# VectorE computes every low part of the weight chunks of a two-layer mixer kernel; GpSimd computes none

## The chip, the cores and the metric

The kernel runs on one core of a Trainium2 chip. Its time is the device time of one launch in microseconds (us), median of several runs. The engines of the core work side by side: TensorE (PE, matrix products into PSUM), VectorE (DVE), ScalarE (ACT), GpSimd (POOL), and SyncE (SP), which here only issues DMAs. A trace lists TensorE's loading of weights apart, as PEld.

## The reference, cut to what matters

Two streams of 256 tokens by 2048 features, `x` and `ctx`, go through two layers; all data is float32. Each layer projects the normalised tokens by wide weight matrices, mixes, and projects back.

```python
def _even_mixer(h_x, h_c, w_in, ..., w_out):            # layer 0
    # projections h @ w_in, then a short convolution and silu of q, k, v
    for d in range(2):                                   # forwards and backwards
        oc_d, s_ctx = _gdn_chunk_scan(q_c, k_c, v_c, ...)     # context first
        ox_d, _ = _gdn_chunk_scan(q_x, k_x, v_x, ..., s_ctx)  # then x, from the context's state
    ...
def _gdn_chunk_scan(q, k, v, g, beta, s0):
    m = strict_lower(kb @ k.T * decay)
    t_inv = inverse(eye + m)                             # per head and chunk: a triangular solve
    ...                                                  # then, chunk by chunk:
    v_new = u_i - w_i @ S;  o = qg_i @ S + a_i @ v_new;  S = S * gl + kg_i.T @ v_new
def _odd_stream(...):                                    # layer 1: gelu, token mixing, pooling
    return concatenate([y_c, y_d]) @ w_out
```

## The kernel before, in words

**High and low parts.** TensorE is fed numbers in a rounded format (fp32r in the trace). To keep float32's precision each operand is split in two: a high part H, the rounded copy, and a low part L, the rest (operand minus H). A projection is then three products: H by H, H by L, and L by H. The activations are split once; the weights arrive from memory in chunks of 128 x 1024 numbers (512 KB; 128 x 768 in the first stage), and each chunk is split when it arrives, by the helper `wchunk`:

```python
raw = (rp or wrawp).tile([P, sz], F32, name="raw", tag="raw")
dma(raw, src)
H = ...tile([P, sz], F32R, name="H", tag="H")
S.copy(H, raw)                                  # L202, ScalarE
L = ...tile([P, sz], F32R, name="L", tag="L")
tick[3] += LP[tick[2]]
if tick[3] >= 1.0:
    tick[3] -= 1.0
    G.tensor_tensor(L, raw, H, ALU.subtract)    # L207, GpSimd
else:
    V.tensor_tensor(L, raw, H, ALU.subtract)    # L209, VectorE
```

`raw`, `H` and `L` have four buffers each. `LP` is a table of shares, one for each stage (`tick[2]` is the stage's number): with 0.5 every second chunk's L goes to GpSimd, with 0.2 every fifth. `RATE` beside it sets how many steps of the layers' modulation vectors (`ada_step`, VectorE's multiply-add L277 with a 256 KB load) come with each chunk.

**The stages.** (0) Normalisation and the first projections (matmuls L450), then keys and values (`wkv`): the matmuls L230, a convolution on VectorE (L351 to L363) whose result TensorE transposes (L599). (1) Four groups of four heads, in one loop. Each group projects q and z, builds per head the matrices U from products E (L747, L749) with VectorE's L757 and L759, then **solves**: 30 steps of elimination on VectorE, each a product (L779, into `ltmp`) and a sum (L781, into `LB`), with transposes around them (L773, L774, L786 to L789) and copies L798 into `UT`. Then the **chain**: TensorE's PT (L807), XT and X (L815, L819, L835, L845) finish the inverse with copies on ScalarE and VectorE between them, and the scan goes through eight steps: z (L883), zk on ScalarE (L887), Sp (L894), the state St on VectorE (L899), kS and QS (L863, L871), r on VectorE (L866), and again z, up to the transposes oT (L922). Beside it, the group's share of sixteen blocks `wbb` is projected (matmuls L230) and convolved. After the fourth group the first part of the output projection starts (L239, L240, L241: H by H, L by H and H by L, 512 columns). (2) The rest of the output projection of layer 0 and the norm. (3) Layer 1.

**What sets the order.** The code is written stage by stage, but a scheduler in the tile framework puts the instructions of each engine in an order of its own before the program is built (`schedule_with_timeline_sim=True`), by its own costs and by what each operation depends on; the solve and the scan have priority (`tc.high_priority()`). On the chip each engine then runs its list strictly in order: an instruction that waits holds up all behind it on the same engine. So the projections' matmuls that stand on TensorE's list between E and PT are what TensorE has to do while VectorE solves.

Of the kernel before, what the change touches and what calls it, by code (L numbers as in the profile page):

```python
# [30 lines left out]
LA = 4  # L31
FINK = 2
RATE = (2.5, 0.6, 1.2, 0.4)
LP = (0.5, 0.5, 0.4, 0.2)
CHUNKS = (1, 2, 4, 4, 5)
RADII = (1, 2, 4, 8)

# [85 lines left out]
def body(ctx: ExitStack, tc: tile.TileContext, T, dbg=None):  # L123
# [71 lines left out]
    def wchunk(src, nk, rp=None, hp=None, lp=None, sz=1024, HL=None):  # L195
# [7 lines left out]
        L = HL[1] if HL else (lp or wlp).tile([P, sz], F32R, name="L", tag="L")  # L203
        tick[3] += LP[tick[2]]
        if tick[3] >= 1.0:
# [989 lines left out]
```

## Time and profile before

| What | Value |
|---|---|
| Median of 3 runs (lowest, highest) | 2234.3 us (2229.0, 2234.8) |
| The profiled execution: time, span of its trace | 2233.2 us, 2231.4 us |
| TensorE busy, share of the span | 2091.3 us, 94% |
| VectorE | 1521.7 us, 68% |
| ScalarE | 995.0 us, 45% |
| GpSimd | 548.3 us, 25% |
| Granted TensorE clock, mean | 0.972 of full speed |
| L on GpSimd (L207) | 205 of 128 x 1024 or less, 508.8 us |
| L on VectorE (L209) | 349, 446.5 us |

Busy time counts the time in which an instruction of the engine was under way, also when that instruction was held up after its start. A share of the whole span is a mean over stages with different limits, so tables over stretches of time are more use than this one. The granted clock tells how much of full speed TensorE had in a stretch.

### The profile page before, as it was taken

To read this page: it belongs to the slowest core of one execution; us is meant where nothing else is said; L and a number is where in the kernel's file an instruction comes from. 1 tells how busy PE (TensorE), PEld (TensorE's weight loads), DVE (VectorE), ACT (ScalarE), POOL (GpSimd) and SP (SyncE) were. 2 spreads that over 40 slices of the span, in tenths; PEclk is the share of its full clock that TensorE was granted. 3 is DMA by queue.
4 is the path that set the end of the run, shared out by engine and by line. 5 is a ranking of instruction groups with operands and counts; after the bars stand their busy time and mean duration, and the time that the engine had idled before them with its cause. 6 is when DMAs were issued, how large, how long until landed. Compare 5 with 4: busy or idle time off the path is not lost. (4 is left out here: it accounts for less than half of the span.)

```text
span 2231.4 us, 42172 instructions
## 1 busy us (share of the span) xinstructions
PE 2091.3 (94%) x17034; PEld 1946.6 (87%) x17034; DVE 1521.7 (68%) x2500; ACT 995.0 (45%) x1726; POOL 548.3 (25%) x258
## 2 busy tenths in 40 slices
PE   6999899999989988998999887999999999999998
PEld 4789899898989988998898876787799999999886
DVE  4337986778965996599569953886767675545445
ACT  5233264225554544563555363445454444444343
POOL 1112111123322332233233321342122112221221
PEclk9999999999999998999899999999999999999999
DMA  9777455767445753564457553896866666666664
GB/s 342 259 264 231 153 166 171 231 210 244 141 133 170 238 187 125 174 210 144 121 187 235 180 166 117 296 317 217 290 202 206 179 184 199 183 191 223 193 194 133
DMA packets 151267, 446.41 MB, mean 200 GB/s; under 512 B 16512, under 2 KB 23456, under 8 KB 150048
## 3 DMA queue, kind: packets, MB, share of 16 engines
q1 hardware_dynamic: 145936, 425.37, 59.4%
q0 software_dynamic: 5136, 18.35, 2.6%
q8 instruction: 133, 2.18, 0.4%
q14 instruction: 62, 0.51, 0.1%
HBM read 423.19 MB, written 20.46 MB: 199 GB/s over the span
## 5 line engine op out<-in xcount | busy, mean ns | idle before, releaser
L202 ACT CAST H<-raw 128x1024 fp32r<-128x1024 f32 (+1 forms) x554 | 573.1, 1042 | 690.1 <-PE pj L230 326.2
L207 POOL TENSOR_TENSOR L<-raw,H 128x1024 fp32r<-128x1024 f32 (+1 forms) x205 | 508.8, 2483 | 1511.1 <-ACT H L202 1426.1
L209 DVE TENSOR_TENSOR L<-raw,H 128x1024 fp32r<-128x1024 f32 (+1 forms) x349 | 446.5, 1281 | 351.3 <-ACT H L202 348.8
L230 PE MATMUL pj<-hxH,L 128*128 128x256 f32 x1856 | 538.1, 290 | 32.5 <-DVE L L209 32.4
L230 PE MATMUL pj<-hxH,H 128*128 128x256 f32 x1856 | 537.0, 289 | 0.1
L230 PE MATMUL pj<-hxL,H 128*128 128x256 f32 x1856 | 536.0, 289 | 0.0
L230 PEld LDWEIGHTS pj<-hxH,L 128*128 128x128 f32 x1856 | 361.7, 195 | 38.7 <-DVE L L209 35.8
L230 PEld LDWEIGHTS pj<-hxL,H 128*128 128x128 f32 x1856 | 361.4, 195 | 2.4 <-issue 1.2
L230 PEld LDWEIGHTS pj<-hxH,H 128*128 128x128 f32 x1856 | 361.3, 195 | 1.8 <-issue 0.9
L230 PE MATMUL pj<-h1H,H 128*128 128x256 f32 x1024 | 291.2, 284 | 0.2 <-DVE yo L1055 0.2
L230 PE MATMUL pj<-h1L,H 128*128 128x256 f32 x1024 | 290.5, 284 | 0.0
L230 PE MATMUL pj<-h1H,L 128*128 128x256 f32 x1024 | 290.3, 284 | 0.0
L277 DVE SCALAR_TENSOR_TENSOR acc<-araw,cs,acc 128x512 f32<-128x512 f32 x240 | 242.8, 1012 | 42.1 <-DMA araw<-in_ada 24.2
L230 PEld LDWEIGHTS pj<-h1H,H 128*128 128x128 f32 x1024 | 197.2, 193 | 0.5 <-PE adc L287 0.3
L230 PEld LDWEIGHTS pj<-h1L,H 128*128 128x128 f32 x1024 | 197.2, 193 | 0.1
L230 PEld LDWEIGHTS pj<-h1H,L 128*128 128x128 f32 x1024 | 197.2, 193 | 0.0
L230 PE MATMUL pj<-hcL,H 128*128 128x256 f32 x320 | 90.9, 284 | 0.0
L230 PE MATMUL pj<-hcH,L 128*128 128x256 f32 x320 | 90.8, 284 | 0.0
L230 PE MATMUL pj<-hcH,H 128*128 128x256 f32 x320 | 90.8, 284 | 0.0
L239 PE MATMUL pj<-H,y1H 128*128 128x512 f32 x192 | 76.0, 396 | 0.0
L241 PE MATMUL pj<-H,y1L 128*128 128x512 f32 x192 | 75.9, 396 | 0.0
L240 PE MATMUL pj<-L,y1H 128*128 128x512 f32 x192 | 75.9, 395 | 0.0
(433 smaller groups left out, 3843.0 us busy)
## 6 DMA issues: line engine op xcount, KB each, us to landing
raw<-in_wbb SPq DMA_DIRECT2D x128, 512.0 KB, 3.9
raw<-in_wout SPq DMA_DIRECT2D x128, 512.0 KB, 4.5
araw<-in_ada SPq DMA_DIRECT2D x192, 256.0 KB, 4.6
raw<-in_ada SPq DMA_DIRECT2D x64, 512.0 KB, 6.3
raw<-in_wpz SPq DMA_DIRECT2D x64, 512.0 KB, 4.1
raw<-in_wuz SPq DMA_DIRECT2D x64, 512.0 KB, 4.1
raw<-in_wkv SPq DMA_DIRECT2D x40, 512.0 KB, 4.4
araw<-in_ada0g SPq DMA_DIRECT2D x64, 256.0 KB, 4.1
```

What stands on the lines that cost most here:

```text
L202: S.copy(H, raw)
L207: G.tensor_tensor(L, raw, H, ALU.subtract)
L209: V.tensor_tensor(L, raw, H, ALU.subtract)
L230: PE.matmul(o[:, e * 256:(e + 1) * 256] if m > 1 else o, w, a[t][:, k, :], start=st and i == 0 and e == 0, stop=sp and i == 2, skip_group_ ...
L239: PE.matmul(o, xH[:, t], H[:, kk, :], start=st, stop=False, skip_group_check=True)
L240: PE.matmul(o, xH[:, t], L[:, kk, :], start=False, stop=False, skip_group_check=True)
L241: PE.matmul(o, xL[:, t], H[:, kk, :], start=False, stop=sp, skip_group_check=True)
L277: V.scalar_tensor_tensor(aacc[u // KT], raw, cs[:, k, 0:1], aacc[u // KT], ALU.mult, ALU.add)
```

## The change

One line: the shares of the table go to zero in all four stages, so `wchunk` takes its second branch for every chunk.

```diff
-LP = (0.5, 0.5, 0.4, 0.2)
+LP = (0.0, 0.0, 0.0, 0.0)
```

All 207 subtractions of GpSimd's list (205 into `L`, two into `h1L`) become subtractions of VectorE's; GpSimd keeps its DMAs (L688, L666, L1108 to L1123, L1147) and six products at the end (L1153). The same numbers are computed. But the scheduler orders all engines anew, since its costs for VectorE's list change.

VectorE, in the solve of the first group: L779 and L781 are the elimination's product and sum (their sizes grow and shrink with the step), L209 the chunks' low parts, L934 and L351 and L352 belong to the convolution of a `wbb` block. Before:

```order
L779 TENSOR_TENSOR ltmp<-LB 128x184
L209 TENSOR_TENSOR L<-raw,H 128x1024
L781 TENSOR_TENSOR LB<-LB,ltmp 128x23x8
L779 TENSOR_TENSOR ltmp<-LB 128x198
L781 TENSOR_TENSOR LB<-LB,ltmp 128x22x9
L779 TENSOR_TENSOR ltmp<-LB 128x210
L934 TENSOR_TENSOR cg<-cg,pj 128x256
L781 TENSOR_TENSOR LB<-LB,ltmp 128x21x10
L779 TENSOR_TENSOR ltmp<-LB 128x220
L351 SCALAR_TENSOR_TENSOR cbt<-cg,cols,cbt 128x4x63
```

VectorE, the same place, now:

```order
L209 TENSOR_TENSOR L<-raw,H 128x1024
L781 TENSOR_TENSOR LB<-LB,ltmp 128x24x7
L779 TENSOR_TENSOR ltmp<-LB 128x184
L781 TENSOR_TENSOR LB<-LB,ltmp 128x23x8
L779 TENSOR_TENSOR ltmp<-LB 128x198
L209 TENSOR_TENSOR L<-raw,H 128x1024
L781 TENSOR_TENSOR LB<-LB,ltmp 128x22x9
L779 TENSOR_TENSOR ltmp<-LB 128x210
L781 TENSOR_TENSOR LB<-LB,ltmp 128x21x10
L209 TENSOR_TENSOR L<-raw,H 128x1024
L779 TENSOR_TENSOR ltmp<-LB 128x220
```

Three or four steps of the elimination stand between two low parts instead of seven to ten. Between the last U (L757) and the first UT (L798) of a group VectorE's list has 8, 10, 9 and 10 low parts in the four groups before, and 21, 29, 23 and 22 now.

TensorE, in the scan of the fourth group (ybH and ybL are activations, H and L the weight chunks of the output projection). Before, the triples L239, L240, L241 stand between the scan's matmuls, up to the last third of the scan:

```order
L241 MATMUL pj<-H,ybL 128x512
L883 MATMUL z<-r,U 128x128 x4
L239 MATMUL pj<-H,ybH 128x512
L240 MATMUL pj<-L,ybH 128x512
L241 MATMUL pj<-H,ybL 128x512
```

TensorE, the same scan, now:

```order
L883 MATMUL z<-Vn,U 128x128 x4
L894 MATMUL Sp<-zk,Kt 128x128
L883 MATMUL z<-Vn,U 128x128 x4
L894 MATMUL Sp<-zk,Kt 128x128 x7
L863 MATMUL kS<-St,KTt 128x128 x4
L883 MATMUL z<-r,U 128x128 x4
L894 MATMUL Sp<-zk,Kt 128x128
L863 MATMUL kS<-St,KTt 128x128 x4
```

From the first PT to oT of the fourth group TensorE's list had 34 matmuls L230 and 192 of L239 to L241 between those of the chain; now it has none. They stand earlier: on TensorE's list between the last E and the first PT of a group there were 455, 536, 454 and 538 matmuls L230, and now there are 584, 753, 609, and in the fourth group 190 of L230 and the 192 of L239 to L241.

## The prediction

> **What bounds the kernel now.** I read the page first, then who TensorE waits for, then stretches of time, then VectorE's list around one wait.
>
> ```profile
> PE 2091.3 (94%) x17034; PEld 1946.6 (87%) x17034; DVE 1521.7 (68%) x2500; ACT 995.0 (45%) x1726; POOL 548.3 (25%) x258
> ```
>
> TensorE carries the span, so a change that touches VectorE and GpSimd alone can only act on what TensorE loses: waits, and stretches at a lower clock. First the waits of TensorE in the four groups but for the last chain (540 to 1290 us), then in all that follows:
>
> ```profile
> PE pj L230 <- DVE L L209: 32.4, 15, 5.1
> PE PT L807 <- DVE UT L798: 15.5, 4, 5.3
> ...
> PE pj L239 <- ACT h1H L345: 2.5, 1, 2.5
> PE pj L240 <- DVE L L209: 2.4, 1, 2.4
> ```
>
> TensorE waits for low parts, but for VectorE's, never for GpSimd's; and after the groups there is next to nothing to gain or to lose, because the waits listed there (1398 to 2232 us) come to 7 us. Now the stretches. Columns: us, then busy us and number of PE, PEld, DVE, ACT, POOL, then granted clock, DMA share and GB/s. In order: keys and values; the solves of the four groups (last E to first PT) with the chain and next projections between them; last the chain of the fourth group.
>
> ```profile
> 240.00:540.00 300.00, 279.05 (x2317) 274.61 (x2315) 236.52 (x433) 124.28 (x275) 64.37 (x28) 0.97 0.60 195
> 567.00:631.00 64.00, 56.40 (x456) 55.58 (x454) 61.40 (x104) 31.99 (x47) 21.86 (x9) 0.96 0.45 149
> 631.00:743.00 112.00, 108.67 (x1283) 106.16 (x1284) 64.15 (x118) 56.02 (x108) 33.23 (x16) 0.96 0.51 158
> 774.00:858.00 84.00, 70.40 (x545) 69.16 (x544) 82.20 (x123) 40.37 (x57) 29.70 (x11) 0.92 0.57 184
> 858.00:965.00 107.00, 104.49 (x1241) 102.32 (x1242) 61.27 (x122) 50.87 (x103) 28.57 (x14) 0.95 0.51 157
> 992.00:1062.00 70.00, 59.45 (x465) 58.10 (x464) 68.17 (x111) 34.50 (x49) 20.70 (x8) 0.93 0.47 151
> 1062.00:1177.00 115.00, 110.33 (x1296) 107.96 (x1297) 69.66 (x128) 55.80 (x110) 35.08 (x16) 0.95 0.53 164
> 1205.00:1289.00 84.00, 68.32 (x546) 67.01 (x544) 82.31 (x124) 37.22 (x55) 28.33 (x11) 0.95 0.57 187
> 1289.00:1398.00 109.00, 93.40 (x913) 80.94 (x916) 48.29 (x100) 49.74 (x94) 24.89 (x11) 0.91 0.44 140
> ```
>
> In the solves VectorE is busy 61.4 of 64, 82.2 of 84, 68.2 of 70 and 82.3 of 84 us: there it is the bound, and TensorE runs out of work. A matmul L230 follows the one before after 0.119 us at full clock, an L239 to L241 after 0.232:
>
> ```profile
> 600.08 0.28 PE L230 MATMUL pj<-hxH,H 128*128 128x256 f32 x1
> 600.20 0.28 PE L230 MATMUL pj<-hxL,H 128*128 128x256 f32 x1
> 600.32 0.28 PE L230 MATMUL pj<-hxH,L 128*128 128x256 f32 x1
> ...
> 1339.42 0.40 PE L239 MATMUL pj<-H,ybH 128*128 128x512 f32 x1
> 1339.66 0.39 PE L240 MATMUL pj<-L,ybH 128*128 128x512 f32 x1
> 1339.89 0.40 PE L241 MATMUL pj<-H,ybL 128*128 128x512 f32 x1
> ```
>
> So the solves hold 54, 65, 55 and 65 us of matmuls, and TensorE loses 10, 19, 15 and 19 us in them. What VectorE does there:
>
> ```profile
> 603.10 1.22 DVE L209 TENSOR_TENSOR L<-raw,H 128x1024 fp32r<-128x1024 f32 x1
> ...
> 606.44 0.41 DVE L781 TENSOR_TENSOR LB<-LB,ltmp 128x234 f32<-128x234 f32 x1
> 606.50 2.57 POOL L207 TENSOR_TENSOR L<-raw,H 128x1024 fp32r<-128x1024 f32 x1 [5.68 <-ACT H L202]
> 606.88 2.44 DVE L779 TENSOR_TENSOR ltmp<-LB 128x228 f32<-128x228 f32 x1
> 609.36 0.40 DVE L781 TENSOR_TENSOR LB<-LB,ltmp 128x228 f32<-128x228 f32 x1
> ```
>
> The product at 606.88 takes 2.44 us, the sum of the same size behind it 0.40: it ends when GpSimd's subtraction does. VectorE's operations with two inputs in SBUF stand still while GpSimd subtracts. What that costs in one solve (774 to 858 us, groups of rows with count, busy us and mean ns), with undisturbed rows behind:
>
> ```profile
> L781 DVE TENSOR_TENSOR LB<-LB,ltmp 128x30 f32<-128x30 f32 (+14 forms) x30 | 17.9, 598 | 0.6
> L779 DVE TENSOR_TENSOR ltmp<-LB 128x30 f32<-128x30 f32 (+14 forms) x30 | 13.9, 462 | 0.8
> L277 DVE SCALAR_TENSOR_TENSOR acc<-araw,cs,acc 128x512 f32<-128x512 f32 x12 | 13.1, 1093 | 0.0
> ...
> 797.50 0.20 DVE L779 TENSOR_TENSOR ltmp<-LB 128x30 f32<-128x30 f32 x1
> 797.95 0.75 DVE L277 SCALAR_TENSOR_TENSOR acc<-araw,cs,acc 128x512 f32<-128x512 f32 x1
> ```
>
> A step has 30 to 240 elements, 165 in the mean; between 0.20 and 0.41 us that is 0.33, so 60 of them take 20 us and took 31.8: 12 us lost; L277 loses 12 x 0.34 = 4 us. Operation by operation against the lower quartile of its own shape, this stretch loses 22 us (the rest lies in copies and convolution steps), the whole trace 228.
>
> **The change, part by part.**
>
> *GpSimd's 207 subtractions go.* None was ever waited for; the gain is what they did to VectorE, 228 us of its time. GpSimd's DMAs (L688, L666, L1121) lose what stood ahead of them on its list; nobody waits for them by the rows above, so 0.
>
> *VectorE gets 207 subtractions.* 1.22 us each, 252 us, less for the 16 small ones. Its sum rises from 1521.7 by some 20 us, and where it is the bound it falls: in the solve shown, eleven low parts moved cost 13.4 us and 22 us of standing still go.
>
> The Trainium skill (Perfetto Trace Analysis, Optimizing Scalar/DVE Operations) says that with VectorE saturated, offloading even to GpSimd may make sense, and adds that it might not help because the two share a read port. The 2.44 us row agrees with the addition; by the first half alone this change would load a saturated engine and end slower, which is the last rival below.
>
> *The first three solves.* VectorE's list between last U and first UT, at undisturbed durations: low parts 21, 29, 23 at 1.22, the elimination with its transposes and copies 32, L277 0, 13, 0 at 0.75, convolution 6, 12, 8: 63, 90 and 67 us. TensorE's matmuls there, 584, 753 and 609 at 0.119: 70, 90 and 72 us. So TensorE has enough to do, with no reserve in the second. It lost 44 us there; I leave 5 us each for low parts that come late, whose releaser would then be H. **-29**; ends -44 (no wait) and 0 (VectorE, whose low parts wait for H in order ahead of the elimination, keeps each wait).
>
> *After the solves.* The clock rows between the solves (0.96, 0.95, 0.95 of 112, 107, 115 us) show 15 us worth lost after the waits for low parts and PT. Half goes: **-8**; ends -15 and 0. But the second group's scan now ends, as the fourth's did, without matmuls between its steps; there the last wait for oT was 6.6 us, in the other groups together 4.1 us:
>
> ```profile
> PE oT L922 <- DVE on L919: 6.6, 1, 6.6
> ...
> PE oT L922 <- DVE on L919: 4.1, 3, 1.8
> ```
>
> **+6**; ends +2 and +8.
>
> *The fourth group.* Its solve: 22 low parts, 27 us, elimination 33, twelve L277 9, others 10, sum 78, and 3.5 of copies UT; the stretch was 84. TensorE has 190 x 0.119 + 192 x 0.232 = 67 us there, so VectorE still ends last: **-2**. The chain took 109 us with 34 x 0.119 + 192 x 0.232 = 49 us of other matmuls in it. Bare it is no shorter than 60, if all its waits were hidden already, and at most 75: the part that was bare took 34 us (first row below: covered, second: bare, with 13 us idle), the covered 75 us less 49 leave 26, and some 15 us of copies, zk, r and St come out from cover.
>
> ```profile
> 1289.00:1364.00 75.00, 72.66 (x771) 61.94 (x772) 32.43 (x51) 35.55 (x53) 20.18 (x9) 0.94 0.49 150
> 1364.00:1398.00 34.00, 20.74 (x144) 18.99 (x145) 15.86 (x49) 14.19 (x41) 4.72 (x2) 0.84 0.35 116
> ```
>
> I take 68, since both directions of the scan now alternate on TensorE's list and fill one another's waits: -41. The 45 us of matmuls that left this group (113 us before, 67 now, last E to oT) are run in the earlier groups and count there in full: **+45**. Ends of the chain with its clock: -8 and +18 around that.
>
> *Keys and values.* 25 low parts cost VectorE 31 us and give back about as much (L277 there has a mean of 1017 ns for 60, so 16 us, the rest elsewhere); VectorE is busy 236 of 300 us. **0**; ends -10 and +10, since TensorE's waits there are for the convolution. Output projection and layer 1: 0. Their cover is VectorE's spare time (rows below: busy 127 of 162 and 392 of 672 us); the 45 low parts moved after 1560 us add 55 us less what stood still, and without that spare time they would cost up to that. The first stage likewise: 0.
>
> ```profile
> L277 DVE SCALAR_TENSOR_TENSOR acc<-araw,cs,acc 128x512 f32<-128x512 f32 x60 | 61.0, 1017 | 17.4 <-DMA araw<-in_ada0g 9.0 <-DMA araw<-in_ada 7.5
> ...
> PE kvp L599 <- DVE kvT L363: 11.9, 6, 4.1
> ...
> 1398.00:1560.00 162.00, 159.17 (x745) 128.22 (x738) 127.31 (x161) 73.53 (x100) 58.58 (x26) 0.99 0.83 278
> 1560.00:2232.00 672.00, 656.39 (x4448) 606.76 (x4446) 392.09 (x520) 287.39 (x368) 133.05 (x73) 0.99 0.65 198
> ```
>
> Sum: -29 - 8 + 6 - 2 - 41 + 45 + 0 = -29, from the profiled execution's 2233.2 (1.8 us over its span, 1.1 under the median): **2204 us**. What is late next is UT, in the fourth group.
>
> **The rivals.**
>
> *No change.* The waits stay and only change their releaser: VectorE's list is in order, and a low part that waits for H holds the elimination behind it; before, half of those waits stood on GpSimd's list, where they hurt nobody. For it: in the second solve 90 us stand against 90. Against it: in the solve of 774 to 858 us VectorE waited for nothing (82.2 busy of 84). Without the 29 and the 8 it is 2233 + 6 - 2 - 41 + 45 = 2241; with a third of the gain, about 2230.
>
> *Slower, by the bare chain.* The chain's place is 1289 to 1398; if it takes 75 us and the clock of the bare stretch (0.84 and less) stretches its 40 us of matmuls by 10, the fourth group is +19 instead of +2, and if the 45 us moved ahead find waits in the earlier solves anyway (none of the 29), the time is 2233 + 19 + 6 = 2258. It decides once the earlier solves give back less than the chain loses, some 25 us. For it: nothing stands between the chain's matmuls. Against it: in the old order cover came in lumps of 21 matmuls that lengthened each step.
>
> *Much faster.* Keys and values also gain, as the scheduler's order meets an undisturbed VectorE: all lower ends together, 2233 - 44 - 15 + 2 - 6 - 10 = 2160. Against it: VectorE's sum there does not fall.
>
> *Slower, by load.* If rows like the 2.44 us one were rare, 39 moved low parts in the four solves would add 39 x 1.22 = 48 us where VectorE is the bound: 2281.
>
> **How the numbers follow.** A measurement of this kernel tells 0.3% from no change, about 7 us. Chances: my forecast (2185 to 2227) 0.47, much faster 0.13, no change 0.17, slower by the bare chain 0.18, by load 0.05. So faster 0.60, same 0.17, slower 0.23. The range leaves out a tenth at either side: 2160 to 2262; the forecast's own is 2185 to 2227.
>
> **What would show it.** Right: L277 falls from 1012 ns to 750 in the mean and VectorE's sum stays within 30 us of 1521.7; TensorE's wait for L209 in the groups falls from 32.4 to under 15 us; the fourth group's chain takes 60 to 75 us at a clock under 0.85, bare of L239. Wrong: waits for low parts whose H came late, an elimination that takes longer than 70 and 90 us, or a chain over 80 us.

## The result, and the profile after

The changed kernel takes **2155.8 us** (median of 4 runs, 2153.4 to 2160.6) where the kernel before, timed beside it, takes 2234.6 (2229.0 to 2237.1). The ratio is **0.965, 95% interval 0.963 to 0.968**: 79 us faster. The forecast was 2204 and the range 2160 to 2262; the direction is the one forecast, the time lies below the range. Two executions that were disturbed, one of the run with the first stage alone (4055 us) and the profiled one of the third lighter solve (5171 us), are left out of the figures below.

First the page's line of busy times of the changed kernel. Its profiled execution has a span of 2153.3 us, 78.1 less than before.

```profile
PE 2062.5 (96%) x17034; PEld 1922.4 (89%) x17034; DVE 1521.6 (71%) x2707; ACT 997.1 (46%) x1726; POOL 34.1 (2%) x51
```

VectorE runs 207 instructions more, and its busy time is the same to 0.1 us: what the low parts add is what the standing still beside GpSimd had cost. TensorE does the same 17034 matmuls in 28.8 us less, since a matmul is shorter at full clock, and it stands idle for 2153.3 - 2062.5 = 90.8 us where it was 140.1. These two, 29 and 49 us, are the whole gain. So the gain is TensorE's lost time, though the change touches neither its work nor its operands.

Whom TensorE waits for, over the whole trace after (total us, times, longest); the last two lines are all that is left of the waits for low parts and for the convolution of keys and values:

```profile
PE PT L807 <- DVE UT L798: 19.2, 6, 14.6
...
PE oT L922 <- DVE on L919: 13.1, 2, 6.6
PE pj L230 <- DVE zb L942: 3.8, 2, 3.0
...
PE pj L240 <- DVE L L209: 0.6, 1, 0.6
...
PE kvp L599 <- DVE kvT L363: 0.6, 1, 0.6
```

Before, the groups alone had 32.4 us for L209, and keys and values 11.9 us for L363. What is late now is UT, most of it in the fourth group (18.2 of the 19.2 us), as the forecast named it.

The stretches of time, with the columns as before (us; busy us and number of PE, PEld, DVE, ACT, POOL; granted clock; DMA share; GB/s). The first row begins where the row of keys and values before began, and ends, as that one did, at the first E. Then come solve and scan of the four groups in turn, and the beginning of layer 1, from TensorE's transposes of its normalised input (L1015) to VectorE's first silu (L1055):

```profile
240.00:516.50 276.50, 275.76 (x2357) 272.95 (x2355) 226.66 (x456) 124.89 (x275) 2.42 (x3) 1.00 0.66 217
545.00:614.00 69.00, 69.00 (x584) 68.83 (x582) 64.71 (x122) 40.19 (x54) 0.00 (x0) 1.00 0.57 171
614.00:722.00 108.00, 104.86 (x1271) 102.75 (x1270) 69.54 (x137) 53.25 (x107) 2.25 (x3) 0.98 0.54 169
750.00:842.00 92.00, 88.98 (x745) 88.65 (x744) 87.43 (x158) 50.93 (x66) 0.00 (x0) 0.98 0.70 219
842.00:938.00 96.00, 85.62 (x1093) 82.68 (x1092) 56.87 (x116) 43.10 (x90) 2.25 (x3) 0.96 0.48 151
966.00:1038.00 72.00, 72.00 (x608) 71.83 (x607) 67.82 (x125) 41.92 (x55) 0.00 (x0) 1.00 0.59 177
1038.00:1149.00 111.00, 106.53 (x1285) 104.28 (x1286) 69.24 (x135) 55.59 (x108) 2.24 (x3) 0.98 0.53 166
1180.00:1265.00 85.00, 67.73 (x366) 57.37 (x364) 75.66 (x132) 39.94 (x48) 0.75 (x1) 0.92 0.66 217
1265.00:1326.00 61.00, 43.11 (x684) 39.71 (x688) 29.22 (x81) 25.99 (x69) 0.00 (x0) 0.81 0.18 58
1464.00:1612.00 148.00, 145.92 (x883) 129.44 (x882) 113.61 (x181) 75.45 (x115) 8.80 (x16) 1.00 0.74 242
```

The last of these was, before:

```profile
1535.00:1690.00 155.00, 148.56 (x899) 130.75 (x897) 118.21 (x175) 77.39 (x120) 34.60 (x25) 1.00 0.72 231
```

Read the first row against its like: keys and values took 300 us with TensorE busy for 279 and now take 276.5 with TensorE busy for 275.8, at full clock. In the first three solves TensorE is busy for 230 of 233 us. By the starts of the same instructions in the two traces, the 78 us lie here:

| From | To | Before, us | After, us | Difference | Forecast |
|---|---|---|---|---|---|
| start | first matmul of keys and values into `kvp` (L599) | 251.0 | 250.7 | 0 | 0 |
| `kvp` | first E (L747) | 288.7 | 265.8 | **-23** | **0** |
| first E | first oT (L922) of the fourth group | 856.2 | 807.6 | **-49** | **-29** |
| oT | first L1015 | 139.4 | 139.9 | 0 | 0 |
| L1015 | first L1055 | 154.3 | 147.7 | **-7** | **0** |
| L1055 | end | 541.9 | 541.6 | 0 | 0 |

VectorE's groups after, then two of before (count, busy us, mean ns, idle before them). The elimination's product and sum fall from 528 and 518 ns to 328 and 329, and the multiply-add L277 from 1012 to 745:

```profile
L277 DVE SCALAR_TENSOR_TENSOR acc<-araw,cs,acc 128x512 f32<-128x512 f32 x240 | 178.8, 745 | 30.9 <-DMA araw<-in_ada 18.4 <-DMA araw<-in_ada0g 10.9
L781 DVE TENSOR_TENSOR LB<-LB,ltmp 128x30 f32<-128x30 f32 (+14 forms) x120 | 39.4, 329 | 2.1
L779 DVE TENSOR_TENSOR ltmp<-LB 128x30 f32<-128x30 f32 (+14 forms) x120 | 39.4, 328 | 2.1
```

```profile
L779 DVE TENSOR_TENSOR ltmp<-LB 128x30 f32<-128x30 f32 (+14 forms) x120 | 63.3, 528 | 3.2
L781 DVE TENSOR_TENSOR LB<-LB,ltmp 128x30 f32<-128x30 f32 (+14 forms) x120 | 62.2, 518 | 2.5
```

### The profile page after: what moved, and what is told of

It is laid out like the page before. It is cut to its first block, busy times and chain, and to the rows that moved or that the text cites. A ratio compares the mean times of both kernels' runs of the same rounds, so it can differ in the third digit from the quotient of the medians.

```text
span 2153.3 us, 42158 instructions
## 1 busy us (share of the span) xinstructions
PE 2062.5 (96%) x17034; PEld 1922.4 (89%) x17034; DVE 1521.6 (71%) x2707; ACT 997.1 (46%) x1726; POOL 34.1 (2%) x51
## 5 line engine op out<-in xcount | busy, mean ns | idle before, releaser
L209 DVE TENSOR_TENSOR L<-raw,H 128x1024 fp32r<-128x1024 f32 (+1 forms) x554 | 667.5, 1207 | 386.0 <-ACT H L202 370.1
L230 PE MATMUL pj<-hxH,H 128*128 128x256 f32 x1856 | 526.8, 284 | 3.8 <-DVE zb L942 3.8
L230 PE MATMUL pj<-hxH,L 128*128 128x256 f32 x1856 | 525.6, 283 | 0.0
L230 PE MATMUL pj<-hxL,H 128*128 128x256 f32 x1856 | 525.3, 283 | 0.0
L230 PEld LDWEIGHTS pj<-hxH,H 128*128 128x128 f32 x1856 | 350.7, 189 | 5.9 <-DVE zb L942 4.1
L230 PEld LDWEIGHTS pj<-hxH,L 128*128 128x128 f32 x1856 | 350.7, 189 | 2.3 <-issue 1.2
L230 PEld LDWEIGHTS pj<-hxL,H 128*128 128x128 f32 x1856 | 350.8, 189 | 0.9
L230 PE MATMUL pj<-h1H,H 128*128 128x256 f32 x1024 | 290.4, 284 | 0.0
L230 PE MATMUL pj<-h1L,H 128*128 128x256 f32 x1024 | 289.8, 283 | 0.0
L230 PE MATMUL pj<-h1H,L 128*128 128x256 f32 x1024 | 289.8, 283 | 0.0
L277 DVE SCALAR_TENSOR_TENSOR acc<-araw,cs,acc 128x512 f32<-128x512 f32 x240 | 178.8, 745 | 30.9 <-DMA araw<-in_ada 18.4
L230 PEld LDWEIGHTS pj<-h1H,H 128*128 128x128 f32 x1024 | 196.5, 192 | 0.2 <-ACT zg L1054 0.2
L230 PEld LDWEIGHTS pj<-h1L,H 128*128 128x128 f32 x1024 | 196.5, 192 | 0.1
L230 PEld LDWEIGHTS pj<-h1H,L 128*128 128x128 f32 x1024 | 196.5, 192 | 0.0
L230 PE MATMUL pj<-hcH,L 128*128 128x256 f32 x320 | 90.4, 283 | 0.0
L230 PE MATMUL pj<-hcH,H 128*128 128x256 f32 x320 | 90.4, 282 | 0.0
L230 PE MATMUL pj<-hcL,H 128*128 128x256 f32 x320 | 90.1, 281 | 0.0
L239 PE MATMUL pj<-H,y1H 128*128 128x512 f32 x192 | 76.0, 396 | 0.0
L241 PE MATMUL pj<-H,y1L 128*128 128x512 f32 x192 | 75.9, 396 | 0.0
L240 PE MATMUL pj<-L,y1H 128*128 128x512 f32 x192 | 75.9, 395 | 0.0
L230 PEld LDWEIGHTS pj<-hcH,L 128*128 128x128 f32 x320 | 60.1, 188 | 0.5 <-issue 0.4
```

Of the source, the lines that this page charges most:

```text
L230: PE.matmul(o[:, e * 256:(e + 1) * 256] if m > 1 else o, w, a[t][:, k, :], start=st and i == 0 and e == 0, stop=sp and i == 2, skip_group_ ...
L239: PE.matmul(o, xH[:, t], H[:, kk, :], start=st, stop=False, skip_group_check=True)
L240: PE.matmul(o, xH[:, t], L[:, kk, :], start=False, stop=False, skip_group_check=True)
L241: PE.matmul(o, xL[:, t], H[:, kk, :], start=False, stop=sp, skip_group_check=True)
L277: V.scalar_tensor_tensor(aacc[u // KT], raw, cs[:, k, 0:1], aacc[u // KT], ALU.mult, ALU.add)
```

## The experiments

"Standing still" below is the sum, over VectorE's operations beside an operation of GpSimd, of what each took beyond the median of its own shape when undisturbed: 228 us before, 4 after. All ratios are to the kernel before, with 95% intervals.

### GpSimd subtracts again, for nobody

This asks whether it is really GpSimd's work that costs, and not the order that the scheduler made of it. VectorE keeps all low parts; for each one that GpSimd used to have in the first stage and the first three groups it also subtracts into scratch (`jon[0]` is false from the fourth group on; the diff is cut).

```diff
+        n = tick[3] >= 1.0                 # tick[3] adds up the shares (0.5, 0.5, 0.4, 0.2)
+        tick[3] -= 1.0 * n
+        if n and jon[0]: G.tensor_tensor(<scratch, 128 x sz>, raw, H, ALU.subtract)
         V.tensor_tensor(L, raw, H, ALU.subtract)
```

> As e1, but GpSimd's useless subtraction is a whole one, as it was before the change (raw minus H, 128 x 1024 or 128 x 768, one instruction), written into a tile that is not in use until the fourth group; so it stands in the first stage and in the first three groups, for the chunks for which GpSimd computed the low part before. VectorE computes every low part. Theory A (standing still in proportion to the time that GpSimd reads): VectorE's multiply-add L277 in keys and values rises from 745 to about 1000 ns in the mean, waits of TensorE for kvT come back to 10 us or more there, the first E of the groups comes at 535 us or later instead of 516, and the time is 2225 to 2290 us, over e1 and, with 252 us more on VectorE, at or over the kernel before. Theory C (order): 2150 to 2190 us.

Measured: 2249.3 us, ratio 1.006 (1.004 to 1.009), so 94 us over the changed kernel in an order much nearer to the changed kernel's than to the one before (TensorE's list has 585, 841, 595 and 407 other matmuls between the last E and the first PT of a group, where the changed kernel has 584, 753, 609 and 382, and the kernel before 455, 536, 454 and 538). The page's line, TensorE's waits, and for 240 to 540 us the stretch and VectorE's multiply-adds:

```profile
PE 2094.2 (93%) x17034; PEld 1946.6 (87%) x17034; DVE 1677.1 (75%) x2707; ACT 993.1 (44%) x1726; POOL 328.7 (15%) x159
```

```profile
PE pj L230 <- DVE L L209: 40.4, 22, 4.8
...
PE kvp L599 <- DVE kvT L363: 15.2, 10, 6.0
```

```profile
240.00:540.00 300.00, 282.52 (x2353) 277.76 (x2352) 269.05 (x461) 123.81 (x274) 73.94 (x29) 0.98 0.60 198
```

```profile
L277 DVE SCALAR_TENSOR_TENSOR acc<-araw,cs,acc 128x512 f32<-128x512 f32 x65 | 67.0, 1031 | 13.1 <-DMA araw<-in_ada0g 7.5 <-DMA araw<-in_ada 5.0
```

294 us of GpSimd's subtractions, of which nobody reads a number, bring back 156 us of VectorE's busy time, the multiply-add at 1031 ns, the waits for low parts and the waits for `kvT`. The standing still is the cause, in keys and values too: the first E starts at 540.4 us (539.7 before, 516.5 in the changed kernel).

### Nobody does GpSimd's share

The other side: what do the 207 subtractions cost on VectorE? The kernel leaves these low parts out and gives TensorE the high part in their place; the diff is cut.

```diff
         if tick[3] >= 1.0:
             tick[3] -= 1.0
-            G.tensor_tensor(L, raw, H, ALU.subtract)
+            L = H
```

> The low parts that GpSimd computed before the change are computed by no engine: for these chunks TensorE is given the high part in place of the low part (the output is not the reference's). So GpSimd is idle as in the changed kernel and VectorE has 207 subtractions, 252 us, less. Theory A: what the change added to VectorE costs little, since VectorE has spare time outside the solves: 2110 to 2150 us, that is 5 to 45 us under the changed kernel, from the last solve and its wait for UT. If the load on VectorE were the price of the change, 2080 us or less. Theory B: about the changed kernel's time less the last wait, 2130 to 2156.

Measured: 2118.2 us, ratio 0.948 (0.946 to 0.951).

```profile
PE 2052.1 (97%) x17034; PEld 1916.1 (91%) x17034; DVE 1297.0 (61%) x2500; ACT 993.9 (47%) x1726; POOL 33.6 (2%) x51
```

VectorE's sum falls by 224.7 us against before, which is the standing still (228). Taking the work off GpSimd is worth 2232 - 2118 = 114 us; doing it on VectorE costs 2156 - 2118 = 38 us, though it is 225 us of work. One us of standing still cost 0.50 us of the time, one us of added subtraction 0.17. The order here is close to that of the kernel before, not to the changed one (460, 537, 448 and 542 matmuls L230 between the last E and the first PT of a group, where the kernel before has 455, 536, 454 and 538). So the 114 us are a gain almost without a new order, and the 38 us hold the new order as well as the subtractions. In keys and values the difference is the plainest: from the first `kvp` to the first E it takes 265.6 us with nobody, 265.8 with VectorE, 286.1 with the useless work on GpSimd and 288.7 before. There the added low parts cost nothing that can be seen.

### One stage at a time

```diff
-LP = (0.5, 0.5, 0.4, 0.2)
+LP = (0.0, 0.5, 0.4, 0.2)      # first stage alone
+LP = (0.5, 0.0, 0.4, 0.2)      # the four groups alone
+LP = (0.5, 0.5, 0.0, 0.0)      # the two last stages alone
```

> Shares 0.0, 0.5, 0.4, 0.2: only the first stage (first projections, keys and values) has its low parts all on VectorE. By the traces the first E of the groups comes 23 us earlier in the changed kernel. Theory A: that gain belongs to this stage alone, TensorE's waits for kvT are gone there: 2200 to 2212 us. If the gain of the stage came from the order of the whole program, it need not appear: 2225 to 2240.

> Shares 0.5, 0.0, 0.4, 0.2: only the four groups have their low parts all on VectorE. Theory A: the waits for low parts in the solves go and those in keys and values stay: 2180 to 2200 us, and with the first stage alone the two gains add up to 70 to 80 us. If the bare chain of the fourth group had cost something that another stage gives back: 2200 to 2230.

> Shares 0.5, 0.5, 0.0, 0.0: only output projection and layer 1 have their low parts all on VectorE. Theory A: what the first stage alone (16 us) and the groups alone (51 us) leave of the change's 77 us, some 5 to 12 us, from the stretch between the output projection and layer 1: 2220 to 2228 us. If nothing was lost there, as TensorE's waits of 7 us said: 2230 to 2236, and the stages do not simply add up.

Measured: 2215.0 (ratio 0.991, 0.988 to 0.994), 2180.5 (0.976, 0.974 to 0.978) and 2228.9 (0.998, 0.996 to 1.000). By the ratios that is about 20, 54 and 5 us, by the medians of the kernel before beside them 17, 51 and 6: together about what the whole change brings. Up to the first E, with the first stage alone and with the groups alone:

```profile
240.00:515.50 275.50, 270.66 (x2298) 267.71 (x2296) 227.72 (x446) 122.27 (x272) 20.55 (x10) 0.99 0.65 210
```

```profile
240.00:545.00 305.00, 287.12 (x2396) 282.41 (x2395) 236.40 (x444) 126.84 (x277) 47.23 (x21) 0.98 0.62 200
```

The first stage's share brings its whole gain by the first E (515.5 us); without it there is none (545.3). In the groups the wait for L209 stays at 28.8 us in the first and is gone in the second, where 2.9 us for low parts are left in the whole trace. The two last stages are worth about 5 us of time (0 to 8 by the interval) and, by L1015 to L1055, 7 of trace (147.7 us in this run, 152.9 and 152.3 in the other two, 154.3 before), where I had put nothing. A new order alone also moves a stretch a little: from the first `kvp` to the first E it takes 291.6 us with the groups alone and 293.2 with the last stages alone, 3 to 5 us over the kernel before, though the first stage's share is the same.

### Useless work in small pieces

Before the run with whole subtractions I had tried pieces of 92 columns, to keep the order of the lists (the diff is cut; a chunk of 1024 columns has six pieces, one of 768 four):

```diff
+        n = sz // 170 if tick[3] >= 1.0 else 0
+        for i in range(n): G.tensor_tensor(junk, raw[:, 92*i:92*(i+1)], H[:, 92*i:92*(i+1)], ALU.subtract)
         V.tensor_tensor(L, raw, H, ALU.subtract)
```

> VectorE computes every low part, as in the changed kernel; beside it GpSimd subtracts again, for the same chunks as before the change, 552 of the 1024 columns in six pieces into a scratch tile that nobody reads. Theory A, standing still (GpSimd's reading holds up VectorE's operations with two inputs in SBUF): VectorE's busy time rises from 1522 us to some 1720 to 1760 us, TensorE waits for low parts and for UT and kvT again, and the time is back at 2225 us or above. Theory B, late low parts (the change gained because a low part is ready after 1.2 us on VectorE instead of 2.5 on GpSimd): nobody waits for the scratch tile, so the time stays at 2150 to 2170 us. Theory C, order (the scheduler's new order gained): 2150 to 2180 us, as the order is nearly the changed kernel's.

Measured: 2201.2 us, ratio 0.986 (0.983 to 0.989); VectorE 1594.0 us busy and 71 us of standing still. Both are well under what I had expected from standing still (1720 to 1760 us busy, and a time of 2225 or above), and the time is above what the two other theories gave (2180 at most).

```profile
L207 POOL TENSOR_TENSOR junk<-raw,H 128x92 fp32r<-128x92 f32 x1198 | 804.9, 672 | 1233.0 <-ACT H L202 600.6 <-issue 533.1 <-DMA raw<-in_ada 16.5
```

GpSimd's 1210 pieces run beside VectorE for 816 us and hurt it less than half as much as 108 whole subtractions of 2.73 us do in 294 us. So it is not the time GpSimd is busy that counts; why small pieces hold VectorE up less stays open. Against the changed kernel 71 us of standing still cost 45 us here (2201 against 2156), and 162 us in the run with whole subtractions cost 94: about 0.6 us for each. The run also answers a rival. A subtraction of GpSimd keeps `raw` and `H` in use until it ends and could so delay the loads; but SyncE's loads waited 407 us for GpSimd here and 52 us in the run with whole subtractions, and that is the slower one.

### Fills in place of subtractions

Does GpSimd hold VectorE up by working, or by reading? The useless subtraction is replaced by a fill of the same scratch (the diff is against that run):

```diff
-        if n and jon[0]: G.tensor_tensor(<scratch, 128 x sz>, raw, H, ALU.subtract)
+        if n and jon[0]: G.memset(<scratch, 128 x sz>, 0.0)
```

> VectorE computes every low part, as in the changed kernel; for each low part that GpSimd had in the first stage and the first three groups it now fills a scratch tile of the same size with zeros (writes only, reads nothing; nobody reads the tile). Theory A, GpSimd's reads are what holds VectorE up: as the changed kernel, 2148 to 2172 us, VectorE busy 1515 to 1545 us, L277 740 to 775 ns in the mean. Theory B, any work of GpSimd on SBUF holds VectorE up while it lasts: VectorE over 1570 us, L277 over 830 ns, and 2185 us or more (the same number of subtractions gave 2249).

Measured: 2161.8 us, ratio 0.967 (0.965 to 0.969), VectorE 1529.7 us. As the fills wait for nobody, all 108 ran in the first 109 us, so the run says nothing on the later stages, and the mean of L277 is no test. But within those 109 us it is one. GpSimd and VectorE's L209 between 3 and 108 us of this run, then the same L209 in the changed kernel:

```profile
L207 POOL MEMSET yo<- 128x1024 f32 (+1 forms) x105 | 100.5, 957 | 6.0
...
L209 DVE TENSOR_TENSOR L<-raw,H 128x768 fp32r<-128x768 f32 x13 | 12.2, 954 | 5.7 <-ACT H L202 5.7
```

```profile
L209 DVE TENSOR_TENSOR L<-raw,H 128x768 fp32r<-128x768 f32 x15 | 14.2, 954 | 11.4 <-ACT H L202 11.4
```

In the run with whole subtractions the same stretch has 15 us of GpSimd's work, and L209 of this shape is slower by half:

```profile
L207 POOL TENSOR_TENSOR yo<-raw,H 128x768 fp32r<-128x768 f32 x7 | 15.1, 2155 | 88.2 <-ACT H L202 77.2 <-issue 11.0
...
L209 DVE TENSOR_TENSOR L<-raw,H 128x768 fp32r<-128x768 f32 x15 | 21.3, 1430 | 9.4 <-ACT H L202 9.4
```

With GpSimd filling for 99 of 105 us the subtraction takes 954 ns, as with GpSimd at rest; with 15 us of GpSimd's reading it takes 1430. So reading does it, for this operation with two inputs.

### Lighter solves

In the changed kernel TensorE still waits 18 us for UT in the fourth group. I gave that solve more matmuls (two other cuts of the sixteen blocks), and then also fewer multiply-adds L277.

```diff
-FCUT = (0, 3, 7, 12, 16)
+FCUT = (0, 3, 6, 11, 16)       # first; (0, 3, 6, 10, 16) in the second
-RATE = (2.5, 0.6, 1.2, 0.4)
+RATE = (2.5, 0.4, 1.6, 0.4)    # in the third only, with the first cut
```

> The changed kernel with other cuts of the sixteen blocks of convolution over the four groups, FCUT (0, 3, 6, 11, 16) instead of (0, 3, 7, 12, 16): 3, 3, 5, 5 blocks instead of 3, 4, 5, 4. On TensorE's list the second group's scan is covered to its end again, and the fourth solve has 572 projection matmuls instead of 382. So of TensorE's waits the 6.6 us for oT in the second group and most of the 18 us for UT in the fourth go, with the low clock after them: 2125 to 2150 us. If the solves are held by VectorE's list alone and not by missing matmuls: 2150 to 2165.

> As f2_cuts with FCUT (0, 3, 6, 10, 16): 3, 3, 4, 6 blocks. The fourth solve has 652 projection matmuls and the first half of its chain has matmuls between its steps again, but the third group's scan ends bare. If bare chains cost what the fourth one's waits say (32 us of waits and a clock of 0.81): 2120 to 2150 us; if the third group's bare end gives it back: as f2_cuts or up to 10 us slower.

> The changed kernel with fewer modulation steps (L277) in the groups (0.4 a chunk in place of 0.6, 1.6 in place of 1.2 in the output projection) and with the sixteen blocks cut at 0, 3, 6, 11, 16. If VectorE's list in the solves still ends after TensorE's matmuls there (fourth group: 76 us against 68), taking some five to nine multiply-adds of 0.75 us out of each solve frees the wait for UT (19 us in all): 2132 to 2150 us, PT's wait under 8 us. Rival: what leaves the solves is paid again in the bare chain or in later waits for the modulation's own data, and the time is 2150 to 2168 us.

Measured: 2152.8 (ratio 0.963, 0.961 to 0.966), 2159.5 (0.966, 0.963 to 0.968), and 2154.4 (0.965, 0.963 to 0.966) for the third, of which no row is shown. None is faster than the changed kernel by what can be told, and none reached what I had hoped for (2125 to 2150, 2120 to 2150 and 2132 to 2150). The first cut's fourth group, waits and chain:

```profile
PE PT L807 <- DVE UT L798: 2.9, 2, 1.9
```

```profile
1254.60:1322.00 67.40, 44.94 (x675) 41.71 (x675) 29.73 (x80) 25.90 (x68) 0.00 (x0) 0.79 0.20 68
```

The wait did go, from 18.2 to 2.9 us, but the bare chain took 67 us in place of 59, with as many matmuls in it (672), and the waits for oT stayed at 13.1 us. Why the chain is longer there stays open.

## Why the prediction was right or wrong, point by point

**Right: the mechanism and its signs.** VectorE's sum, forecast to stay within 30 us of 1521.7, is 1521.6; L277 fell to 745 ns (forecast 750); the wait for L209 in the groups, forecast under 15, is gone; the chain of the fourth group runs bare at a clock of 0.81 (and in 59 us, just under the 60 to 75 named). The useless subtractions show that standing still is the cause, and the run in which nobody does GpSimd's share shows the gain in nearly the old order.

**Wrong: keys and values at 0; -23 us measured.** This is the step that failed. It set the 31 us of added low parts against "about as much" given back and concluded that equal sums have equal effects. The first half holds roughly: VectorE's sum there went from 237 to 227 us, so it gave back 41 us for the 31. The second does not. The added low parts fitted into VectorE's spare time (some 60 of 300 us): the stretch takes 265.8 us with them and 265.6 without. A stall falls on whatever is running, and what stands behind it on the list is late, the convolution `kvT` among them, for which TensorE waits. The row quoted in the prediction held the size all along: TensorE was idle for 21 of 300 us and its clock was at 0.97. I set that loss aside because "TensorE's waits there are for the convolution". The convolution's operations that read PSUM were indeed not slowed (L352 478 ns before, 475 after). What was held up stood ahead of `kvT` on VectorE's list. One such place of the trace before: beside GpSimd's subtraction the convolution's L354 takes 0.48 us, but the multiply-add behind it takes 2.11 instead of 0.75, and TensorE then waits 1.76 us for `kvT`:

```profile
431.92 2.40 POOL L207 TENSOR_TENSOR L<-raw,H 128x1024 fp32r<-128x1024 f32 x1 [9.47 <-ACT H L202]
...
432.37 0.48 DVE L354 SCALAR_TENSOR_TENSOR ct<-pj,conv,ct 128x255 f32<-128x255 f32 x1
...
432.76 2.11 DVE L277 SCALAR_TENSOR_TENSOR acc<-araw,cs,acc 128x512 f32<-128x512 f32 x1
...
437.22 0.68 DVE L363 SCALAR_TENSOR_TENSOR kvT<-cth,ct 128x512 f32<-128x512 f32 x1
...
438.05 0.41 PE L599 MATMUL kvp<-cst,kvT 128*128 128x128 f32 x2 [1.76 <-DVE kvT L363]
```

So the waits were for an engine that was held up *ahead* of the operation waited for. The name of the releaser says who was last, not who was slow.

**Mis-sized: the first three solves, -29; -42 by the stretches.** The low end, -44, was the right one. VectorE's lists were sized well (forecast 63, 90 and 67 us, measured 64.7, 87.4 and 67.8), and TensorE lost 0, 3 and 0 us. The 5 us left in each "for low parts that come late" had no row behind them; no low part came late. Another 3 us or so came from the E's ahead of the solves.

**Mis-sized: the bare chain, -41; -48.** It took 59 us against 107 by the starts of PT and oT, where 68 was taken and 60 called the least. The forecast had added 34 us, 26 us and some 15 us of copies and states that were to come out from cover; 59 us are the first two alone, so none of the 15 shows.

**About right.** The scans after the solves: groups one and three became 4 us shorter each, the second's bare end cost 6 (-8 and +6 forecast). The fourth solve: -2 forecast, 0 found; UT is late there as said. The matmuls moved ahead: +45 forecast, and the stretches close with it: -45 - 8 + 6 + 0 - 48 + 45 = -50, against -49 by the table.

**Missed: L1015 to L1055, -7.** VectorE's spare time was named there as cover for added work; that GpSimd's 0.2 and 0.4 shares also held it up there was left out. TensorE's idle time fell from 6.4 to 2.1 us.

In sum, -23, -16, -7 and -7 us that were not foreseen, and +2 for the fourth solve, take 2204 to 2153, 2 us under the profiled execution.

**The rivals.** "Much faster" (2160, keys and values gain too) is what happened, and what was held against it, that VectorE's sum there does not fall, was wrong as a fact (it fell by 10 us) and as a rule. "No change" falls with the waits for L209. "Slower by load" falls with the run in which nobody does the share: 38 us is all that 225 us more of VectorE cost. "Slower by the bare chain" falls with 59 us. The Trainium skill (Perfetto Trace Analysis, Optimizing Scalar/DVE Operations) names both sides, offloading from a saturated VectorE and the shared read port that may undo it; the runs here agree with the second by 79 us.

## What to carry to other kernels

A stall and an addition of the same length on the same engine do not cost the same: here a us of standing still cost 0.5 us of the time, and a us of plain work put where the scheduler found room cost 0.17, what the new order cost included. So price a shared resource by the idle time of the bounding engine in that stretch, whoever is named as the releaser, and not by the balance of the helper engine's busy time. And before giving elementwise work with two inputs in SBUF to GpSimd, compare VectorE's mean durations beside it and away from it: a few rows of one operation at two lengths are the warning.

## What the runs showed of the hardware

**Which of VectorE's operations a fill holds up.** While GpSimd filled scratch, between 14 and 29 us, the scaling L428, whose one large input and output both lie in SBUF, was about twice as long, though the two-input L209 was not touched. With the fills, then in the changed kernel, forms apart:

```profile
L428 DVE TENSOR_SCALAR tok<-tok,rst 128x1536 f32<-128x1536 f32 x4 | 7.0, 1780 | 0.0
L428 DVE TENSOR_SCALAR tok<-tok,rst 128x512 f32<-128x512 f32 x4 | 4.1, 1067 | 0.1
```

```profile
L428 DVE TENSOR_SCALAR tok<-tok,rst 128x1536 f32<-128x1536 f32 x4 | 3.9, 1014 | 0.0
...
L428 DVE TENSOR_SCALAR tok<-tok,rst 128x512 f32<-128x512 f32 x4 | 1.8, 483 | 0.1
```

The Trainium skill (SBUF — State Buffer, Who interferes with whom) says that a VectorE operation with two SBUF inputs contends with a GpSimd operation that reads SBUF but not with one that only writes it, while scalings and copies in the modes that use both port pairs contend with either. The runs agree on all three counts: 2.44 us beside a subtraction, 954 ns beside a fill, and 1067 against 483 ns for the scaling. The 7.6 us by which the first `kvp` came later in that run (258.2 against 250.7) lie in this opening part.

**A short wait can cost clock.** In the trace before, a wait of 1.88 us for a low part (836.96 us) is followed by one stretch at half clock, in which 18 matmuls run where the next has 31:

```profile
836.96 0.38 PE L230 MATMUL pj<-hxH,L 128*128 128x256 f32 x1 [1.88 <-DVE L L209]
```

```profile
833.60:837.20 3.60, 1.72 (x15) 1.51 (x14) 3.53 (x7) 1.06 (x1) 0.41 (x1) 1.00 0.41 94
837.30:840.70 3.40, 3.40 (x18) 3.40 (x17) 3.16 (x8) 1.05 (x1) 0.84 (x1) 0.50 0.84 265
840.70:844.10 3.40, 3.40 (x31) 3.40 (x30) 3.37 (x4) 1.06 (x1) 1.55 (x1) 1.00 0.31 124
```

It is not so after every such wait: after 1.76 us at 438.05 and 2.37 us at 1613.02 the clock stays at 1.00 for the next 9 us. The mean clock went from 0.972 to 0.985. Taken as time at full speed that is 0.028 x 2231 = 62 us lost before and 0.015 x 2153 = 32 after, 30 us less. That fits the 29 us by which the matmuls became shorter beside the 49 us of idle time that went.
